# Hybrid decoder layer: the score products with the keys' low parts as pairs of 64-row matmuls

## The chip, the cores and the metric

The kernel runs on one core of a Trainium2 chip. The time is the device time of one execution in microseconds (us); where several executions are shown, the median is meant.

## The reference

One layer over 1040 positions (16 learned meta positions ahead of 1024 inputs), width 1024. After a norm and one input projection, head group B is a sliding-window attention (window 128) with 8 query heads of 64 channels over 2 key heads, and a sink value per head; group A is a convolution and a gated linear recurrence. Then come an output projection and a feed-forward block of width 4096. Cut to what matters here:

```
z = u @ w_in;  q, k, v, xr, yr = split(z)
s = einsum("bnqkgd,bnskd->bnkgqs", qb, kk) * 64**-0.5      # blocks of 128 queries x 256 keys
s = where(valid, s, -1e30);  m = max(max(s), sink)
p = exp(s - m);  o = einsum(..., p / (sum(p) + exp(sink - m)), vv)
a, gates:  r = sigmoid(einsum(x_blocks, w_a)), i = sigmoid(einsum(x_blocks, w_x))   # 8 blocks of 64 x 64
h = h + rmsnorm(concat(o, rec) @ w_out);  h = h + rmsnorm(relu(u @ w_ff1)**2 @ w_ff2)
```

## The kernel before

**Numbers in two parts.** TensorE (PE) works on rounded float32 (`F32R`). To keep accuracy, each operand is held as a high part (rounded) and a low part (what the rounding lost), and a product is made of high times high, high times low and low times high. The helper `mm3` records these as its three lines L125, L130 and L131, so most PE rows of the profile carry one of those lines.

**Queries and keys.** The heads are taken in pairs `j` of 0 to 3: query head `j` with key head 0 and query head `j + 4` with key head 1, `h` being 0 or 1. Key head `h` lies in partitions `HALF[h]` (0 to 63, or 64 to 127). For each pair and each `h`, the tile `q[h]` holds the high part of the query in `HALF[h]` and its low part in the other half. The tile `khh[h]` holds the high part of key head `h` in both halves (a DMA at L532 copies it across), so that one matmul over 128 rows gives high times high plus low times high. The tile `kl[h]` (L294) holds the low part of key head `h` in `HALF[h]` and zeros in the other half (two memsets on GpSimd, L297), so that a second matmul over 128 rows, with the same `q[h]`, adds high times low alone. `km` is a small tile of the same parts for block 0: slots 0 and 1 are high parts, slots 2 and 3 low parts with zeros (memsets L411, L412). The functions `low_k` and `sink_k` fill all these as the key projection leaves PSUM.

**Scores.** `scores(j, half, q)` computes 4 blocks of 128 queries against 256 keys for both `h`. For each `h`, and for each of two pairs of blocks `bp`, it takes a PSUM bank with the tag "s" (two banks have it), and puts into it for each of two blocks `i` the matmul of L625 (with `khh`) and that of L629 (with `kl`), each with a 128 x 128 stationary part of `q[h]` and 256 moving columns. ScalarE (ACT) and VectorE (DVE) take the bank out (L642, L643). After both `bp` of an `h` come its minimum (L652), four exponentials, the reciprocal and the scaling (L661). It runs 8 times, 4 `j` by 2 `half`: 64 matmuls of L625 and 64 of L629. `attend` then transposes the probabilities (L675) and multiplies them by the values (L691).

**What sets the order.** The program is written as one stream; a scheduler with its own timeline puts each engine's instructions in order, by priorities and the times that it expects. The remaining input projections (`next_fill`, of the `mm3` lines) are recorded with a lower priority (`deferred(FILL_LAG)`), so that the scheduler spreads them between the matmuls of scores and attention. At run time every engine keeps the order that was fixed. Tiles with one tag share a fixed number of buffers (17 for "b", in which `khh`, `kl`, `q` and later operands lie).

**Gates.** Later, `gates` multiplies 64-channel blocks: at L817 two matmuls, one with its operands in partitions 0 to 63, one in 64 to 127, write to two PSUM banks, three products in each of three column pieces (348, 348 and 344 columns), for four chunks `c`.

Of the kernel before, what the change touches and what calls it, by code (L numbers as in the profile page):

```python
# [10 lines left out]
F32R = mybir.dt.float32r  # L11
AF = mybir.ActivationFunctionType
ALU = mybir.AluOpType
# [3 lines left out]
P = 128  # L17
D = 1024
KC = D // P
T = 1024  # L20
NMETA = 16
# [16 lines left out]
def hybrid_layer(  # L38
# [6 lines left out]
    nc = tc.nc  # L45
# [12 lines left out]
    def slot(tag, shape, dt=F32):  # L58
        uid[0] += 1
        return slab.tile(shape, dt, tag=tag, name=f"{tag}{uid[0]}", bufs=bufs[tag])  # L60
# [4 lines left out]
    def bank(tag, shape=(P, 512)):  # L65
        uid[0] += 1
        return ps.tile(list(shape), F32, tag=tag, name=f"ps_{tag}{uid[0]}")

    def f32(ap):
        return ap.bitcast(F32)  # L70
# [10 lines left out]
    def lut(*args, **kwargs):  # L81
        ins = nc.scalar.activation(*args, **kwargs).ins  # L82
        if last_lut[0] is not None:
            tc.add_manual_dep(
                ins, last_lut[0],
                mybir.DependencyInfo(
                    mybir.DependencyClass.NoSync, mybir.DependencyReason.DATA
                ),
                reason="lut",
            )  # L90
        last_lut[0] = ins.name
        return ins
# [198 lines left out]


    khh = [slot("b", [P, T], F32R) for _ in range(2)]
    kl = [slot("b", [P, T], F32R) for _ in range(2)]  # L294
    HALF = (slice(0, HD), slice(HD, P))
    for h in range(2):
        nc.gpsimd.memset(f32(kl[h][HALF[1 - h]]), 0.0)  # L297

    zeros = slot("ws", [P, 512], F32R)
    nc.vector.memset(f32(zeros), 0.0)  # L300
# [30 lines left out]
    def chained(e, ins):  # L331
        if last[e] is not None:
            behind(last[e], ins)
        last[e] = ins.name
# [73 lines left out]
    wq = high_w(rq)  # L408
    low_w(wq, rq)
    km = slot("ws", [P, 4, 2 * P], F32R)  # L410
    nc.gpsimd.memset(f32(km[:, 0:2, 0 : P - NMETA]), 0.0)  # L411
    nc.gpsimd.memset(f32(km[:, 2:4, :]), 0.0)  # L412
    nsink = const.tile([P, 8], F32, name="nsink")
    nc.sync.dma_start(nsink, attn_sinks[0].partition_broadcast(P))
    prm_r = slot("d", [8, 512])
# [16 lines left out]
    def high_k(hh, src):  # L432
        return [nc.scalar.copy(hh[h][HALF[h]], src[HALF[h]]).ins for h in range(2)]

    def low_k(hh, lo, src):
        return [
            nc.vector.tensor_tensor(
                lo[h][HALF[h]], src[HALF[h]], f32(hh[h][HALF[h]]), op=ALU.subtract
            ).ins
            for h in range(2)  # L440
        ]

    def sink_k(acc, t0, n):
        o = NMETA if t0 == 0 else 0
        c = slice(t0 + o - NMETA, t0 - NMETA + n)
        parts = [([khh[0][:, c], khh[1][:, c]], [kl[0][:, c], kl[1][:, c]], acc[:, o:])]
        if o:

            m, mk = slice(0, NMETA + P), slice(P - NMETA, 2 * P)
            parts.append(  # L450
                ([km[:, 0, mk], km[:, 1, mk]], [km[:, 2, mk], km[:, 3, mk]], acc[:, m])
            )
        ops = [[], []]
        for hh, lo, src in parts:
            ops[0] += high_k(hh, src)
        for hh, lo, src in parts:
            ops[1] += low_k(hh, lo, src)
        if o:
            for e in range(2):
                for ins in ops[e]:  # L460
                    chained(e, ins)
# [36 lines left out]
    for b in range(4):  # L498
# [3 lines left out]
        if b == 0:  # L502

            acc = [bank("acc"), bank("acc")]
            for a, w in zip(acc, (wk, wv)):
                part(a, w, piece, 0)
                part(a, w, piece, 1)
            xn = [(norm_rows(xt[2], P, True), P)]
            xn.append((norm_rows(xt[3], P, True), P))
            part(acc[0], wk, piece, 2)  # L510
            sink_k(acc[0][:, : piece[1]], *piece)
            part(acc[1], wv, piece, 2)
            sink_v(acc[1][:, : piece[1]], *piece)
            wx = high_w(rx)
            low_w(wx, rx)
            for w, (t0, n), sink, tag in (
                (wq, (16, 256), sink_q0, "o"), (wx, piece, sink_x0, "acc"),
            ):
                acc = bank(tag)
                for k in range(3):  # L520
                    part(acc, w, (t0, n), k)
                sink(acc[:, :n], t0, n)
            done.append(last_mm[0])
            continue
        project(wk, [piece], sink_k)
        project(wv, [piece], sink_v)
        project(wq, [piece], sink_q0)
        project(wx, [piece], sink_x0)
        done.append(last_mm[0])
    for h in range(2):  # L530
        r, o, m = HALF[h], HALF[1 - h], slice(P - NMETA, 2 * P)
# [62 lines left out]
    for b in range(2):  # L594
        pv = bank("pt", (P, 4, P))
        for i in range(4):
            o = NMETA + (4 * b + i) * P
# [11 lines left out]
    def scores(j, half, q):  # L609

        sn = slot("c", [P, 2, 4, P + 1])
        negm = small.tile([P, 2, 4], F32, name="negm", tag="negm")
        den = small.tile([P, 2, 4], F32, name="den", tag="den")
        rden = small.tile([P, 2, 4], F32, name="rden", tag="rden")
        for h in range(2):
            nc.gpsimd.tensor_copy(
                sn[:, h, :, P], nsink[:, j + 4 * h : j + 4 * h + 1].to_broadcast([P, 4])
            )
        for h in range(2):
            for bp in range(2):  # L620
                sp_ = bank("s", (P, 2, 256))

                def qk(dst, b, hi, lo):
                    c = slice(b * P, (b + 1) * P)
                    nc.tensor.matmul(  # L625
                        dst, q[h][:, c], hi, start=True, stop=False,
                        skip_group_check=True,
                    )
                    nc.tensor.matmul(  # L629
                        dst, q[h][:, c], lo, start=False, stop=True,  # L630
                        skip_group_check=True,
                    )

                for i in range(2):
                    b = 4 * half + 2 * bp + i
                    if b == 0:
                        qk(sp_[:, i, :], b, km[:, h, :], km[:, 2 + h, :])
                    else:
                        c = slice((b - 1) * P, (b + 1) * P)
                        qk(sp_[:, i, :], b, khh[h][:, c], kl[h][:, c])  # L640
                s_ = sn[:, h, 2 * bp : 2 * bp + 2, 0:P]
                nc.scalar.copy(s_, sp_[:, :, P:256])  # L642
                nc.vector.copy_predicated(  # L643
                    s_, above_i.rearrange("p (a b) -> p a b", a=1).to_broadcast([P, 2, P]),
                    sp_[:, :, 0:P],
                )
                if half == 0 and bp == 0:
                    w = slice(0, P - NMETA)
                    nc.vector.copy_predicated(
                        sn[:, h, 0, w], above_i[:, w], far.to_broadcast([P, P - NMETA])  # L650
                    )
            nc.vector.tensor_reduce(  # L652
                negm[:, h, :], sn[:, h], axis=mybir.AxisListType.X, op=ALU.min
            )
            for k in range(4):
                lut(
                    sn[:, h, k, :], sn[:, h, k, :], AF.Exp, scale=-1.0,
                    bias=negm[:, h, k : k + 1], accum_out=den[:, h, k : k + 1],
                )
            nc.vector.reciprocal(rden[:, h, :], den[:, h, :])  # L660
            nc.vector.tensor_tensor(  # L661
                sn[:, h, :, 0:P], sn[:, h, :, 0:P],
                rden[:, h, :].to_broadcast([P, 4, P]), op=ALU.mult,
            )
        return sn
# [109 lines left out]
    for j in range(NPAIR):  # L775
        for half in range(2):
            if j % 2 == 0 and half == 0:
                at_pair(j // 2)
            gate_after = last_lut[0]
            sn = scores(j, half, qs[j])  # L780
            if True:
                with deferred(FILL_LAG):
                    next_fill()
            if prev is not None:
                attend(*prev)
            prev = (j, half, sn)
# [652 lines left out]
    def col_parts(i, j):  # L1439
        return HALVES if i == 6 and j == 3 else COLS[:1]  # L1440
# [32 lines left out]
    for j in range(4):  # L1473
        parts = col_parts(6, j)
# [34 lines left out]
```

## Time and profile before

| | us |
|---|---|
| median of 3 executions | 958.47 |
| the three | 956.39, 958.47, 961.83 |
| span of the profiled execution, first to last instruction | 955.3 |
| PE busy in it | 943.8 |
| PE weight loads (PEld) busy | 789.7 |
| DVE busy | 655.7 |
| ACT busy | 505.9 |
| GpSimd (POOL) busy | 129.1 |

For the profiled execution the profile gives the span and no separate time; the median of the shown executions is 3.2 us above that span. In a row of the timeline the first number is the start in us from the span's start, the second the duration in us, then the engine, the line, the operation, what it writes and reads, for matmuls the rows and columns of the stationary part (128\*128, 64\*128), and the shape of the moving operand. Matmuls are pipelined, so that rows overlap: what one costs PE is read from start to start, not from its duration.

### The profile page before, as it was taken

The page shows a single profiled execution, that of the slowest core. Times are in us where ns is not written, and L with a number is a line of the kernel's source. Part 1 is how long each engine was busy: PE and PEld are TensorE (multiplying, and loading weights), DVE is VectorE, ACT ScalarE, POOL GpSimd, SP SyncE. Part 2 cuts the span into 40 slices and gives each one's busy share as a digit, 9 for nine tenths or more (in the row PEclk, how much of TensorE's full clock was granted, in tenths as well). Part 3 has the DMA queues.
Part 4 walks back from the last instruction along what each step waited for, and adds up shares of the span by engine and source line. Part 5 has one row for each costly group of instructions (what it writes and reads, how often), then busy time and mean ns, then how long its engine had stood idle before and what let it go on. Part 6 is the DMA issues. An engine that isn't in the chain of part 4 may idle for free.

```text
span 955.3 us, 12432 instructions
## 1 busy us (share of the span) xinstructions
PE 943.8 (99%) x4728; PEld 789.7 (83%) x4728; DVE 655.7 (69%) x845; ACT 505.9 (53%) x854; POOL 129.1 (14%) x189
## 2 busy tenths in 40 slices
PE   9999999999999999999999999999999999999996
PEld 8999999877888878888888888888887788888885
DVE  6567987788856787665644465476667576779893
ACT  7537766568645554444655575654433343446441
POOL 4102563520021100010000000001121100001201
PEclk9999999999999999999999999999999999999999
DMA  8221010204226368674422364334777765647934
GB/s 271 56 67 23 24 45 24 67 23 131 83 109 185 133 220 264 198 253 144 155 89 88 111 203 127 104 113 114 175 180 186 185 199 177 192 139 196 246 65 89
DMA packets 88199, 130.21 MB, mean 136 GB/s; under 512 B 13702, under 2 KB 52630, under 8 KB 88140
## 3 DMA queue, kind: packets, MB, share of 16 engines
q1 hardware_dynamic: 78972, 104.44, 34.0%
q0 software_dynamic: 8880, 24.19, 12.2%
q8 instruction: 37, 0.61, 0.3%
q10 hardware_dynamic: 288, 0.79, 0.2%
q14 instruction: 22, 0.18, 0.1%
HBM read 109.93 MB, written 18.87 MB: 135 GB/s over the span
## 4 chain that ended last, share of the span: by engine, by line
PE 88%; DVE 5%; ACT 3%; DMA 2%; POOL 1%; issue 1%; SPq 0%; DVEq 0%; ACTq 0%; POOLq 0%
PE ps_acc L130 10%; PE ps_acc L131 10%; PE ps_acc L125 10%; PE ps_s L131 6%; PE ps_s L130 6%; PE ps_s L125 6%; PE ps_pt L130 6%; PE ps_pt L131 6%; PE ps_pt L125 6%; PE ps_o L130 5%; PE ps_o L131 5%; PE ps_o L125 5%; ACT c L82 1%; PE ps_o L691 1%; PE ps_acc L282 1%
## 5 line engine op out<-in xcount | busy, mean ns | idle before, releaser
L99 DVE TENSOR_TENSOR ws<-raw,ws 128x1024 fp32r<-128x1024 f32 (+1 forms) x69 | 82.6, 1197 | 76.1 <-ACT ws L96 24.3
L96 ACT CAST ws<-raw 128x1024 fp32r<-128x1024 f32 (+1 forms) x68 | 69.7, 1026 | 87.9 <-PE ps_o L130 23.9
L96 ACT CAST ws<-e 128x1024 fp32r<-128x1024 f32 x41 | 43.0, 1049 | 82.8 <-PE ps_o L130 35.3
L125 PE MATMUL ps_acc<-a,ws 128*128 128x256 f32 (+2 forms) x256 | 85.8, 335 | 0.0
L130 PE MATMUL ps_acc<-a,ws 128*128 128x256 f32 (+2 forms) x256 | 85.5, 334 | 0.0
L131 PE MATMUL ps_acc<-a,ws 128*128 128x256 f32 (+2 forms) x256 | 85.0, 333 | 0.0
L99 DVE TENSOR_TENSOR b<-b,b 128x1024 fp32r<-128x1024 f32 (+2 forms) x50 | 58.9, 1177 | 24.8 <-PE ps_o L130 19.1
L96 ACT CAST b<-b 128x1024 fp32r<-128x1024 f32 (+2 forms) x49 | 49.9, 1019 | 46.4 <-DVE b L996 41.0
L99 DVE TENSOR_TENSOR ws<-e,ws 128x1024 fp32r<-128x1024 f32 x41 | 50.1, 1223 | 32.4 <-ACT ws L96 18.9
L680 POOL TENSOR_SCALAR_AFFINE_SELECT c<-c 128x512 fp32r<-128x512 f32 x64 | 53.6, 858 | 67.6 <-ACT c L96 59.3
L125 PEld LDWEIGHTS ps_acc<-a,ws 128*128 128x128 f32 x256 | 48.3, 189 | 4.7 <-issue 0.2
L131 PEld LDWEIGHTS ps_acc<-a,ws 128*128 128x128 f32 x256 | 48.3, 189 | 4.5
L130 PEld LDWEIGHTS ps_acc<-a,ws 128*128 128x128 f32 x256 | 48.2, 188 | 4.4 <-issue 0.4
L125 PE MATMUL ps_acc<-ws,b 128*128 128x512 f32 (+1 forms) x120 | 46.3, 387 | 1.1 <-ACT ws L96 1.1
L130 PE MATMUL ps_acc<-ws,b 128*128 128x512 f32 (+1 forms) x120 | 46.3, 386 | 0.5 <-DVE ws L99 0.4
L131 PE MATMUL ps_acc<-ws,b 128*128 128x512 f32 (+1 forms) x120 | 46.1, 385 | 0.0
L125 PE MATMUL ps_pt<-ws,b 128*128 128x512 f32 x112 | 44.4, 396 | 0.0
L130 PE MATMUL ps_pt<-ws,b 128*128 128x512 f32 x112 | 44.1, 394 | 0.0
L131 PE MATMUL ps_pt<-ws,b 128*128 128x512 f32 x112 | 44.0, 393 | 0.0
L125 PE MATMUL ps_s<-ws,b 128*128 128x512 f32 x110 | 43.4, 395 | 0.0
L131 PE MATMUL ps_s<-ws,b 128*128 128x512 f32 x110 | 43.3, 394 | 0.0
L130 PE MATMUL ps_s<-ws,b 128*128 128x512 f32 x110 | 43.3, 393 | 0.0
(416 smaller groups left out, 2662.0 us busy)
## 6 DMA issues: line engine op xcount, KB each, us to landing
raw<-in_w_ff_dram SPq DMA_DIRECT2D x61, 512.0 KB, 4.1
e<-in_w_ff_dram SPq DMA_DIRECT2D x45, 512.0 KB, 4.0
a<-in_w_ff_dram SPq DMA_DIRECT2D x12, 512.0 KB, 6.6
s_dram<-a POOLq DMA_DIRECT2D x12, 512.0 KB, 3.7
c<-in_x_dram SPq DMA_DIRECT2D x8, 512.0 KB, 4.0
raw<-in_w_in_dram SPq DMA_DIRECT2D x8, 512.0 KB, 3.7
d<-in_x_dram SPq DMA_DIRECT2D x8, 512.0 KB, 3.3
out_dram<-raw SPq DMA_DIRECT2D x8, 512.0 KB
```

The source lines that it names most:

```text
L82: ins = nc.scalar.activation(*args, **kwargs).ins
L96: nc.scalar.copy(hi, src)
L99: low = nc.vector.tensor_tensor(lo, src, f32(hi), op=ALU.subtract).ins
L125: ins = nc.tensor.matmul(dst, lh, rh, start=start, stop=False, skip_group_check=True).ins
L130: nc.tensor.matmul(dst, lh, rl, start=False, stop=False, skip_group_check=True)
L131: last_mm[0] = nc.tensor.matmul(dst, ll, rh, start=False, stop=stop, skip_group_check=True).ins.name
L282: last_mm[0] = nc.tensor.matmul(acc[:, :n], w[k // 2][:, kc, :], u[kc][k % 2][:, t0 : t0 + n], start=k == 0 and kc == 0, stop=k == last an ...
L680: nc.gpsimd.affine_select(out=p_[:, :, s], in_=f32(p_[:, :, 0]), pattern=[[0, 4], [g, P]], compare_op=op, fill=0.0, base=0, channel_multip ...
L691: nc.tensor.matmul(po[:, oc : oc + n], v, p_[:, pc : pc + n], start=first and k == 0, stop=last and k == 1, skip_group_check=True,)
```

## The change

There is now one tile `kl`, with the low parts of both key heads, each in its own half, and no zeros; `km` needs three slots, the third with both low parts. In `scores` both `h` are handled together for each `bp`: two banks are taken, and for each block the order written is two matmuls with the high parts (128 rows, one for each `h`), then two with the low parts over 64 rows, from `HALF[0]` and `HALF[1]`, into the two banks. The two banks are then taken out, and the rest of the softmax follows in a second loop over `h`, after both `bp` of both heads. Three of the four memsets go; one of them becomes one slot longer.

```
-    kl = [slot("b", [P, T], F32R) for _ in range(2)]
+    kl = slot("b", [P, T], F32R)
     HALF = (slice(0, HD), slice(HD, P))
-    for h in range(2):
-        nc.gpsimd.memset(f32(kl[h][HALF[1 - h]]), 0.0)
...
-    nc.gpsimd.memset(f32(km[:, 0:2, 0 : P - NMETA]), 0.0)
-    nc.gpsimd.memset(f32(km[:, 2:4, :]), 0.0)
+    nc.gpsimd.memset(f32(km[:, 0:3, 0 : P - NMETA]), 0.0)
...
-                lo[h][HALF[h]], src[HALF[h]], f32(hh[h][HALF[h]]), op=ALU.subtract
+                lo[HALF[h]], src[HALF[h]], f32(hh[h][HALF[h]]), op=ALU.subtract
...
-        for h in range(2):
-            for bp in range(2):
-                sp_ = bank("s", (P, 2, 256))
...
+        for bp in range(2):
+            sps = [bank("s", (P, 2, 256)) for _ in range(2)]
+            for i in range(2):
+                b = 4 * half + 2 * bp + i
+                cq, ck = slice(b * P, (b + 1) * P), slice((b - 1) * P, (b + 1) * P)
+                for h in range(2):
                     nc.tensor.matmul(
-                        dst, q[h][:, c], hi, start=True, stop=False,
-                        skip_group_check=True,
+                        sps[h][:, i, :], q[h][:, cq],
+                        khh[h][:, ck] if b else km[:, h, :],
+                        start=True, stop=False, skip_group_check=True,
                     )
+                for h in range(2):
+                    r = HALF[h]
                     nc.tensor.matmul(
-                        dst, q[h][:, c], lo, start=False, stop=True,
-                        skip_group_check=True,
+                        sps[h][:, i, :], q[h][r, cq], kl[r, ck] if b else km[r, 2, :],
+                        start=False, stop=True, skip_group_check=True,
                     )
...
+            for h in range(2):
+                sp_ = sps[h]
                 s_ = sn[:, h, 2 * bp : 2 * bp + 2, 0:P]
                 nc.scalar.copy(s_, sp_[:, :, P:256])
...
+        for h in range(2):
             nc.vector.tensor_reduce(
                 negm[:, h, :], sn[:, h], axis=mybir.AxisListType.X, op=ALU.min
             )
```

In the changed kernel the matmuls with the high parts are L622 and those with the low parts L629.

More of the change, by code (lines that the diff above doesn't have):

```diff
@@ L445, in sink_k @@
         c = slice(t0 + o - NMETA, t0 - NMETA + n)
-        parts = [([khh[0][:, c], khh[1][:, c]], [kl[0][:, c], kl[1][:, c]], acc[:, o:])]
+        parts = [([khh[0][:, c], khh[1][:, c]], kl[:, c], acc[:, o:])]
         if o:
@@ L450, in sink_k @@
             parts.append(
-                ([km[:, 0, mk], km[:, 1, mk]], [km[:, 2, mk], km[:, 3, mk]], acc[:, m])
+                ([km[:, 0, mk], km[:, 1, mk]], km[:, 2, mk], acc[:, m])
             )
@@ L618, in scores @@
             )
-        for h in range(2):
-            for bp in range(2):
-                sp_ = bank("s", (P, 2, 256))
-                def qk(dst, b, hi, lo):
-                    c = slice(b * P, (b + 1) * P)
+        for bp in range(2):
[4 more added lines that the diff above has]
+                for h in range(2):
                     nc.tensor.matmul(
-                        dst, q[h][:, c], hi, start=True, stop=False,
-                        skip_group_check=True,
-                    )
+                        sps[h][:, i, :], q[h][:, cq],
+                        khh[h][:, ck] if b else km[:, h, :],
+                        start=True, stop=False, skip_group_check=True,
+                    )
+                for h in range(2):
+                    r = HALF[h]
                     nc.tensor.matmul(
-                        dst, q[h][:, c], lo, start=False, stop=True,
-                        skip_group_check=True,
-                    )
[L634 to L640, printed above, removed]
+                        sps[h][:, i, :], q[h][r, cq], kl[r, ck] if b else km[r, 2, :],
+                        start=False, stop=True, skip_group_check=True,
+                    )
+            for h in range(2):
+                sp_ = sps[h]
                 s_ = sn[:, h, 2 * bp : 2 * bp + 2, 0:P]
```

## The prediction

> **What bounds the kernel now.** I read the page first: how busy each engine is, the clock granted to PE, and the chain of work that ended last.
>
> ```profile
> span 955.3 us, 12432 instructions
> ...
> PE 943.8 (99%) x4728; PEld 789.7 (83%) x4728; DVE 655.7 (69%) x845; ACT 505.9 (53%) x854; POOL 129.1 (14%) x189
> ...
> PEclk9999999999999999999999999999999999999999
> ...
> PE 88%; DVE 5%; ACT 3%; DMA 2%; POOL 1%; issue 1%; SPq 0%; DVEq 0%; ACTq 0%; POOLq 0%
> ```
>
> PE is busy for 943.8 of 955.3 us at full clock, and holds 88% of the chain. A busy share is no proof, since matmul rows overlap, so I ask who made PE wait (the waits of PE; us in total, times, longest; the three that count).
>
> ```profile
> PE ps_acc L308 <- DVE base_e L562: 1.5, 1, 1.5
> PE ps_acc L125 <- ACT ws L96: 1.1, 1, 1.1
> ...
> PE ps_o L691 <- POOL c L680: 0.3, 1, 0.3
> ```
>
> The first is the program's start, the second is in the feed-forward part, and only the third, 0.3 us, is in the attention. The windows place the rest: scores and attention, everything behind the gates up to PE's last matmul, and the tail.
>
> ```profile
> core 0: us, PE busy (x) PEld busy (x) DVE busy (x) ACT busy (x) POOL busy (x), PEclk, DMA share, GB/s
> 59.70:196.00 136.30, 135.98 (x931) 125.60 (x930) 111.55 (x188) 87.65 (x251) 56.58 (x76) 1.00 0.16 43
> ...
> 212.00:948.10 736.10, 734.27 (x3246) 597.02 (x3244) 492.74 (x550) 372.79 (x500) 51.67 (x71) 1.00 0.53 156
> 948.10:955.30 7.20, 0.03 (x1) 0.00 (x0) 2.83 (x7) 0.20 (x1) 0.43 (x1) 0.77 0.71 159
> ```
>
> In the 136.30 us that hold the scores PE is idle for 0.32, and in the 736.10 us behind the gates for 1.83. So PE time that the change adds or removes in the scores moves the end by about as much: what can absorb an addition is at most 0.3 + 1.8 = 2.1 us, and I take it as nothing, since each of these waits has its own cause behind it.
>
> **The low products as they are.** One head's four block products in the timeline, the first two, the last, and the transpose that follows:
>
> ```profile
> 79.98 0.28 PE L625 MATMUL ps_s<-b,b 128*128 128x256 f32 x1
> 80.09 0.28 PE L629 MATMUL ps_s<-b,b 128*128 128x256 f32 x1
> ...
> 80.81 0.28 PE L629 MATMUL ps_s<-b,b 128*128 128x256 f32 x1
> 80.92 0.27 PE L675 MATMUL ps_pt<-ident,c 128*128 128x128 f32 x1
> ```
>
> Eight products take 80.92 - 79.98 = 0.94 us, 0.118 each. The 64 products of L629 cost 64 x 0.118 = 7.5 us, and if all ran as 32 pairs, two at once, 3.8 us would be saved. That is the most that pairing can bring, and it is under 0.5% of the time (4.8 us), about what a measurement of this kernel can tell from no change.
>
> **What a 64-row pair costs.** The kernel already has such pairs, in the gates (L817). One chunk, with the full-height projections (512 columns) on both sides:
>
> ```profile
> 209.19 0.39 PE L130 MATMUL ps_acc<-a,ws 128*128 128x512 f32 x1
> 209.42 0.39 PE L131 MATMUL ps_acc<-a,ws 128*128 128x512 f32 x1
> 209.74 0.43 PE L817 MATMUL ps_s<-b,e 64*128 64x348 f32 x1
> 209.75 0.43 PE L817 MATMUL ps_pt<-b,e 64*128 64x348 f32 x1
> 210.01 0.32 PE L817 MATMUL ps_s<-b,e 64*128 64x348 f32 x1
> ...
> 211.11 0.32 PE L817 MATMUL ps_pt<-b,e 64*128 64x344 f32 x1
> 211.12 0.32 PE L817 MATMUL ps_o<-b,e 64*128 64x344 f32 x1
> 211.37 0.50 PE L125 MATMUL ps_acc<-a,ws 128*128 128x512 f32 x1
> 211.71 0.39 PE L130 MATMUL ps_acc<-a,ws 128*128 128x512 f32 x1
> 211.94 0.39 PE L131 MATMUL ps_acc<-a,ws 128*128 128x512 f32 x1
> ```
>
> The pairs are real: both start within 0.01 us, and from the second pair (210.01) to the ninth (211.11) are seven steps of 0.157 us. A full-height product of 348 columns would cost, on a line through 0.118 at 256 columns and 0.23 at 512 (209.19 to 209.42), 0.158. So two 64-row products take the time of one full one, and a pair of 256 columns should take 0.118.
>
> The switch between full height and half height is what costs. From 209.42 to 211.71 are 2.29 us. The work in them is one 512-column product, nine pairs and one more 512-column product: 0.23 + 9 x 0.157 + 0.23 = 1.87. The rest, 0.42 us, is one way in and one way out. The first pair could have started at 209.65 and started at 209.74, and its rows are 0.43 long instead of 0.32; on the way out a start was due at 211.27, came at 211.37, and the row is 0.50 instead of 0.39. Each switch is thus about 0.10 us in which nothing starts, and 0.11 us in which the weights load with no product beside them. The weight loads show the second part:
>
> ```profile
> 209.74 0.18 PEld L817 LDWEIGHTS ps_s<-b,e 64*128 64x128 f32 x1 [0.36 <-ACT c L82]
> ...
> 209.85 0.19 PEld L817 LDWEIGHTS ps_s<-b,e 64*128 64x128 f32 x1
> ```
>
> After idling, the first load keeps its half of the array for 0.11 us before the next follows, at which time the first product streams. (The wait on ACT named there is older than the idle time: the product before ran until then.)
>
> The Trainium skill speaks against this change at this point: TensorEngine Tiling (Array Packing), Key Properties, says that changing the tiling mode, and not just the tile, drains the TensorE. It gives no duration; the 0.10 us in which nothing starts agree with it. TensorE: Matmul & The Clock Gate, LDWEIGHTS (loading the stationary operand), puts a load at its columns divided by 1.2, in ns; an estimate for 128 columns is 0.107 us. With that load alone at each switch the sum below would be 51 x 2 x 0.107 - 1.5 = 9.4 us.
>
> **How often it switches.** The diff writes two high, two low; the scheduler decides what stands where. In the order of the changed program (L622 high, L629 low; `b_268` and `b_269` are the two heads' queries):
>
> ```
> 513 L622 Matmult ps_s_1002<-b_109,b_268 128x256
> 514 L629 Matmult ps_s_1002<-b_111,b_268 128x256
> 515 L622 Matmult ps_s_1003<-b_110,b_269 128x256
> 516 L629 Matmult ps_s_1003<-b_111,b_269 128x256
> 517 L622 Matmult ps_s_1002<-b_109,b_268 128x256
> 518 L622 Matmult ps_s_1003<-b_110,b_269 128x256
> 519 L629 Matmult ps_s_1002<-b_111,b_268 128x256
> 520 L629 Matmult ps_s_1003<-b_111,b_269 128x256
> ```
>
> The second block is a pair; in the first the scheduler put each low product right behind its high one, alone between full-height products. Over all 64 low products there are 51 runs: 13 pairs of two different halves and 38 products alone. A product alone over 64 rows streams the same 256 columns and saves nothing.
>
> **The sum on PE.** 51 runs x 0.42 = +21.4 us (0.415 by the unrounded steps: +21.2); 13 pairs x 0.118 = -1.5. That is +19.6 us. The trace has no run of one product between full-height ones. Its bounds: below, the loads alone (0.11 at each switch), 51 x 0.22 - 1.5 = +9.7; above, the whole 0.42, +19.9. I take the upper row, since both parts of it come from the change of height and not from the number of products between.
>
> **What else moves.** The removed memsets are at the start:
>
> ```profile
> 1.12 0.95 POOL L297 MEMSET b<- 64x1024 f32 x1
> 2.40 0.94 POOL L297 MEMSET b<- 64x1024 f32 x1
> ...
> 4.72 0.57 POOL L176 TENSOR_TENSOR rs<-ms,half_pow 16x1 f32<-16x1 f32 x1
> 5.25 0.69 DVE L242 CUSTOM_DVE_ANT_0 d<-c 128x512 f32<-128x512 f32 x1 [3.77 <-DMA c<-in_x_dram]
> 5.86 0.74 DVE L260 TENSOR_SCALAR d<-d,rs 16x1024 f32<-16x1024 f32 x1
> ...
> 8.36 0.53 POOL L412 MEMSET ws<- 128x512 f32 x1
> ```
>
> The meta rows' norm (L176) ends at 5.29, and its reader on DVE (L260) stands behind L242, which waits for a DMA and holds DVE to 5.86. So an earlier L176 gives nothing: the DMA covers it, and 0. The memset at 8.36 has no reader on PE before the scores. The smaller `kl` frees one of 17 "b" buffers; among PE's waits none is for a buffer, so 0 again, at most the 2.1 us of idle time. DMA issues on SP stand in the same order; the other queues change only inside the attention.
>
> The new wait is in the softmax: head 0 can no longer start while head 1 is multiplied, and both finish together. The durations (x count, busy us, mean ns):
>
> ```profile
> L643 DVE COPY_PREDICATED c<-above,ps_s 128x256 f32<-128x256 int32 x32 | 13.0, 448 | 0.6 <-ACT c L642 0.2
> L661 DVE TENSOR_TENSOR c<-c,rden 128x512 f32<-128x512 f32 x15 | 11.0, 731 | 0.4
> L652 DVE TENSOR_REDUCE negm<-c 128x4 f32<-128x516 f32 x16 | 11.0, 685 | 0.5
> ...
> L82 ACT ACTIVATE c<-c,negm 128x129 f32<-128x129 f32 x64 | 25.0, 395 | 3.7 <-DVE negm L652 3.5
> ...
> L642 ACT COPY c<-ps_s 128x256 f32<-128x256 f32 x32 | 10.5, 373 | 2.6 <-PE ps_s L629 2.5
> ```
>
> From the last score product to the first transpose both heads need, if little overlaps, 0.37 + 2 x 0.45 + 2 x 0.69 + 8 exponentials at most 0.39 each + 2 x 0.73 = 7.3 us. In the changed order, with the steps above (0.118, 0.23, the switches), PE has at least 8.1 us of other work between the two in every one of the 8 score steps. The margin is 0.8 us, with DVE busy 111.55 of 136.30 us, so a wait is possible: 0 to about 0.6 us in each of 8 steps, 0 to 5 us. I take 0.
>
> **The rivals.**
> - *Only the weight load is exposed.* If the 0.10 us without a start came from changing a long stream of nine pairs and not from a single product, the sum is +9.7: 968. Against it: the delay is as long into the pairs as out of them.
> - *The softmax of two heads at once makes PE wait.* +19.6 and up to 5 more, 983. For it is the small margin; against it, PE is slower here, which gives ACT and DVE time.
> - *Not slower: the switch is hidden.* If the load for the other half slips under a running product, only 13 x 0.118 = 1.5 us of savings are left: 957. It decides where a way in and out costs less than 0.03 us; up to (4.8 + 1.5) / 51 = 0.12 us it stays within 0.5%. The Trainium skill, TensorE: Matmul & The Clock Gate, Part 3, has a rule for it: loads overlap products in flight where the row group differs. The gates' 0.42 us show that it does not hold between full and half height, since a full-height product uses every row.
> - *The change does not do what it says:* 38 of 64 low products do not stand in pairs. This is part of my sum.
>
> **How the numbers follow.** The sum is against the span of 955.3, which would be 974.9; the median shown is 3.2 above that span, so I forecast 958.5 + 19.6 = 978. Chances: forecast 0.75; load alone 0.10; softmax waits 0.08; hidden switch 0.05; a gain over 0.5% 0.02, for what I do not see, since pairing brings 3.8 at most. The range 970 to 984 takes in a somewhat cheaper switch (0.28 us a run gives 971) and the softmax waits, and leaves out 0.17. Slower by over 0.5%: 0.75 + 0.10 + 0.08 = 0.93; within it 0.05; faster 0.02.
>
> **What would show it.** In the timeline after, a full-height product behind a lone low product should stream some 0.53 us (0.118 + 0.42) after that low product was due, with rows 0.11 us longer at each switch, and the window from the first score to the gates should be about 20 us longer, everything behind it the same. The forecast is wrong if that distance is near 0.12 us, if 64-row rows do not lengthen, or if the longer time lies in PE waits on ACT or DVE.

## The result and the profile after

The changed kernel takes 973.51 us (median of 4, 973.35 to 974.25) against 958.0 us (median of 4, 956.39 to 961.83) for the kernel before. The ratio is 1.017, with a 95% interval of 1.0149 to 1.019. It is slower by 15.5 us, inside the range and 4.5 us under the forecast.

The page of the changed kernel, the same lines as before:

```profile
span 971.9 us, 12425 instructions
...
PE 962.1 (99%) x4728; PEld 794.7 (82%) x4728; DVE 656.8 (68%) x845; ACT 507.9 (52%) x854; POOL 119.4 (12%) x186
...
PEclk9999999999999999999999999999999999999999
...
PE 92%; DVE 3%; DMA 2%; ACT 1%; issue 1%; DVEq 0%; SPq 0%; ACTq 0%
```

PE is busy 18.3 us longer (962.1 against 943.8) at the same clock, with the same 4728 matmuls; its part of the chain rises from 88% to 92%. DVE and ACT do what they did, within 2 us, and POOL is 9.7 us less busy (119.4 against 129.1), with three memsets fewer and 64 mask operations of 732 ns instead of 858 on average. The list of PE's waits is shorter than before, and none of them is in the attention:

```profile
PE ps_acc L306 <- DVE base_e L559: 1.5, 1, 1.5
PE ps_acc L125 <- ACT ws L96: 0.6, 1, 0.6
PE ps_pt L130 <- DVE a L99: 0.2, 1, 0.2
```

To place the time I cut both traces at the same matmuls: the 441st (which both programs have at the same place, 0.6 us ahead of the first score product before), the first of the gates, and PE's last. The windows before:

```profile
59.13:196.62 137.49, 137.17 (x938) 126.38 (x937) 112.14 (x192) 87.90 (x251) 56.67 (x77) 1.00 0.16 43
196.62:947.80 751.18, 749.35 (x3352) 609.06 (x3352) 505.12 (x563) 382.48 (x521) 55.70 (x73) 1.00 0.52 153
```

and after (columns: length, then the busy time of PE, PEld, DVE, ACT, POOL, clock, DMA):

```profile
58.57:213.71 155.14, 155.14 (x938) 130.92 (x936) 113.32 (x192) 89.57 (x251) 49.06 (x77) 1.00 0.14 38
213.71:964.30 750.59, 749.64 (x3352) 609.24 (x3352) 505.38 (x563) 382.80 (x521) 55.44 (x73) 1.00 0.53 154
964.30:971.90 7.60, 0.29 (x3) 0.08 (x1) 2.83 (x7) 0.20 (x1) 0.68 (x1) 0.86 0.74 160
```

Scores and attention take 155.14 us instead of 137.49, +17.65, with the same 938 matmuls. The scores start 0.56 us earlier, the part behind them is 0.59 shorter, the tail 0.1 longer: +16.6, the difference of the spans. (The 938 are all matmuls that touch the window; 936 start in it.) One of the score steps in the timeline shows the cost (128\*128 is full height, 64\*128 half height; "x2" is two products):

```profile
74.24 0.28 PE L622 MATMUL ps_s<-b,b 128*128 128x256 f32 x1
74.45 0.39 PE L629 MATMUL ps_s<-b,b 64*128 64x256 f32 x1
74.76 0.39 PE L622 MATMUL ps_s<-b,b 128*128 128x256 f32 x1
75.08 0.38 PE L629 MATMUL ps_s<-b,b 64*128 64x256 f32 x1
75.39 0.50 PE L622 MATMUL ps_s<-b,b 128*128 128x256 f32 x2
75.82 0.39 PE L629 MATMUL ps_s<-b,b 64*128 64x256 f32 x2
76.14 0.50 PE L125 MATMUL ps_acc<-a,ws 128*128 128x512 f32 x1
76.47 0.39 PE L130 MATMUL ps_acc<-a,ws 128*128 128x512 f32 x1
```

Where high and low alternate, the steps are 0.31 us (74.45, 74.76, 75.08, 75.39) instead of 0.118: each change of height costs 0.19. It has two parts that can be read from the rows. The low product was due at 74.36 and starts at 74.45, and its row is 0.39 long where the high one's is 0.28. The weight loads go with this. Between full-height products, here before the change, the load for the product at 62.15 starts 0.11 us ahead of it, with the product before:

```profile
62.04 0.28 PE L131 MATMUL ps_acc<-a,ws 128*128 128x256 f32 x1
62.04 0.19 PEld L125 LDWEIGHTS ps_acc<-a,ws 128*128 128x128 f32 x1
62.15 0.28 PE L125 MATMUL ps_acc<-a,ws 128*128 128x256 f32 x1
```

At a change of height, after the change, the load starts only with its own product (at 74.45 and 74.76):

```profile
74.44 0.18 PEld L629 LDWEIGHTS ps_s<-b,b 64*128 64x128 f32 x1 [0.25 <-issue]
74.76 0.19 PEld L622 LDWEIGHTS ps_s<-b,b 128*128 128x128 f32 x1
```

The pair at 75.82 streams in the time of one product, as in the gates, but pays the same way in and out.

### The profile page after: what moved, and what is told of

Same layout as the page of the kernel before. It is cut to its first block, busy times and chain, and to the rows that moved or that the text cites. A ratio compares the mean times of both kernels' runs of the same rounds, so it can differ in the third digit from the quotient of the medians.

```text
span 971.9 us, 12425 instructions
## 1 busy us (share of the span) xinstructions
PE 962.1 (99%) x4728; PEld 794.7 (82%) x4728; DVE 656.8 (68%) x845; ACT 507.9 (52%) x854; POOL 119.4 (12%) x186
## 4 chain that ended last, share of the span: by engine, by line
PE 92%; DVE 3%; DMA 2%; ACT 1%; issue 1%; DVEq 0%; SPq 0%; ACTq 0%
PE ps_acc L130 11%; PE ps_acc L131 11%; PE ps_acc L125 11%; PE ps_s L131 6%; PE ps_s L130 6%; PE ps_s L125 6%; PE ps_pt L130 6%; PE ps_pt L131 6%; PE ps_pt L125 6%; PE ps_o L130 5%; PE ps_o L131 5%; PE ps_o L125 5%; PE ps_o L686 2%; PE ps_s L629 2%; PE ps_s L622 1%; PE ps_acc L282 1%
## 5 line engine op out<-in xcount | busy, mean ns | idle before, releaser
L99 DVE TENSOR_TENSOR ws<-raw,ws 128x1024 fp32r<-128x1024 f32 (+1 forms) x69 | 82.8, 1200 | 75.8 <-ACT ws L96 24.7
L96 ACT CAST ws<-raw 128x1024 fp32r<-128x1024 f32 (+1 forms) x68 | 69.8, 1026 | 86.4 <-PE ps_o L130 26.9
L96 ACT CAST ws<-e 128x1024 fp32r<-128x1024 f32 x41 | 43.0, 1049 | 81.6 <-PE ps_o L130 34.0
L99 DVE TENSOR_TENSOR b<-b,b 128x1024 fp32r<-128x1024 f32 (+2 forms) x50 | 58.9, 1178 | 24.8 <-PE ps_o L130 19.1
L96 ACT CAST b<-b 128x1024 fp32r<-128x1024 f32 (+2 forms) x49 | 50.0, 1020 | 46.8 <-DVE b L991 41.4
L99 DVE TENSOR_TENSOR ws<-e,ws 128x1024 fp32r<-128x1024 f32 x41 | 50.1, 1222 | 32.3 <-ACT ws L96 18.9
L675 POOL TENSOR_SCALAR_AFFINE_SELECT c<-c 128x512 fp32r<-128x512 f32 x64 | 45.1, 732 | 95.1 <-ACT c L96 92.6
```

The source lines that it names most:

```text
L96: nc.scalar.copy(hi, src)
L99: low = nc.vector.tensor_tensor(lo, src, f32(hi), op=ALU.subtract).ins
L675: nc.gpsimd.affine_select(out=p_[:, :, s], in_=f32(p_[:, :, 0]), pattern=[[0, 4], [g, P]], compare_op=op, fill=0.0, base=0, channel_multip ...
```

## The experiments

Two theories. "Switch": every run of half-height products between full-height ones costs PE a fixed time for the way in and out, whatever is in it. "Order": the time comes from the new loops, with both heads at once, the softmax starting later, and another order by the scheduler. For each kernel stand the total, and the window from the 441st matmul to the first gate, in which PE's busy time is set against the 137.17 us of before.

**Full height in the new order.** The loops of the changed kernel stay, and the zeros come back:

```
+    kl = [slot("b", [P, T], F32R) for _ in range(2)]     # zeros in the other half
...
-    sps[h][:, i, :], q[h][r, cq], kl[r, ck] if b else km[r, 2, :],
+    sps[h][:, i, :], q[h][:, cq], kl[h][:, ck] if b else km[:, 2 + h, :],
```

> The changed kernel with its loops and PE order kept, its low products put back to full height with zeros in the other half (64 products alone or in pairs at the same 51 places). Theory 'switch' (each run of half-height products costs PE about 0.39 us for the way in and out, whatever is computed): nothing of the 16 us is left, 957 to 959 us, and PE's steps in the scores are 0.118 us throughout. Rival 'order' (both heads at once, the softmax starting later and the scheduler's new order cost the time): as slow as the changed kernel, 972 to 975 us.

Measured: 957.12 us (956.2 to 959.65) against 956.0 for the kernel before in the same session, ratio 1.0011 (0.9999 to 1.0023). All matmuls stand in the order of the changed kernel, and the instructions of ACT and DVE too. Its window, a step of the same form as 75.39 to 76.14 above, and its longest PE wait in the attention:

```profile
58.91:197.38 138.47, 137.34 (x938) 126.17 (x936) 112.04 (x192) 88.79 (x251) 49.43 (x77) 1.00 0.16 43
```

```profile
65.84 0.48 PE L625 MATMUL ps_s<-b,b 128*128 128x256 f32 x2
66.16 0.40 PE L631 MATMUL ps_s<-b,b 128*128 128x256 f32 x2
66.40 0.39 PE L125 MATMUL ps_acc<-a,ws 128*128 128x512 f32 x1
```

```profile
PE ps_acc L125 <- DVE b L479: 0.9, 1, 0.9
```

Two low products take 0.24 us, and PE's busy time is back to 137.34. This kernel differs from the changed one in the height of 64 products, the second tile of low parts and the memsets, and its window is 16.7 us shorter (138.47 against 155.14). "Order" falls; what is left of it is a PE wait of 0.9 us on DVE, which the slower products had covered. The tile and the memsets go with the height here, but all kernels below have one tile and no zeros, like the changed one, and PE's busy time grows by 3.7 to 24.4 us in them, with the number of runs. So the height is the cause.

**Half height in the old order.** The loops of before, with the shared tile, and each low product behind its own high one:

```
-    dst, q[h][:, c], lo, start=False, stop=True,
+    dst, q[h][HALF[h], c], lo, start=False, stop=True,
```

> The kernel before with its loops, but one tile of low parts and half-height low products: each of the 64 stands alone behind its high product, so there are 64 runs and no pair. 'Switch': 64 x 0.39 = +25.0 us and about -0.5 at the start without the memsets, 982 to 983 us. 'Order': the loops are those of before, so 957 to 959 us. A third theory, that a half-height product costs something only where two write two banks at once and a lone one is cheaper: under 974 us.

Measured: 979.85 us (978.59 to 982.15), ratio 1.0251 (1.0234 to 1.0267), +23.9, where +24.5 was expected. (The total is 2 us under the range expected, which counted from 958, while the kernel before, timed beside it, took 956.0.) Its window, and the first steps of a score group:

```profile
58.84:220.44 161.60, 161.60 (x938) 134.03 (x936) 115.47 (x192) 90.25 (x251) 52.32 (x77) 1.00 0.14 37
```

```profile
66.22 0.38 PE L626 MATMUL ps_s<-b,b 64*128 64x256 f32 x1
66.53 0.39 PE L622 MATMUL ps_s<-b,b 128*128 128x256 f32 x1
66.85 0.38 PE L626 MATMUL ps_s<-b,b 64*128 64x256 f32 x1
67.16 0.39 PE L622 MATMUL ps_s<-b,b 128*128 128x256 f32 x1
```

No pair is in it, and it is the slowest: a lone half-height product pays in full. The third theory falls too.

**All 32 pairs together.** The low products are ordered behind the second high one of their block:

```
+    low = nc.tensor.matmul(...).ins
+    behind(high.name, low)
```

> The changed kernel with each low product ordered behind the second high product of its block, so that all 32 pairs stand together (32 runs of two). 'Switch': 32 x 0.39 - 32 x 0.118 = +8.7 us, with -0.5 at the start 966 us (965 to 968). 'Order': the loops and the softmax are as late as in the changed kernel, 972 to 975 us.

Measured: 965.14 us (964.36 to 966.87), ratio 1.0097 (1.008 to 1.0114), +9.1. Its window:

```profile
58.84:204.98 146.14, 145.90 (x940) 126.44 (x938) 112.53 (x191) 88.24 (x251) 51.33 (x77) 1.00 0.15 41
```

This is the form that the change's words describe, and it is still slower: a pair saves 0.118 us and pays more than three times that.

**Runs of four.** The high products of both blocks first, then the low ones of both:

```
             for i in range(2):
                 ...  # both high products
+            for i in range(2):
                 for h in range(2):
                     low = ...
+                    behind(high.name, low)
```

> The changed kernel with the low products of two blocks ordered behind their last high product: 19 runs, 14 of them of two pairs, 3 of one pair, 2 of one product. 'Switch': 19 x 0.39 - 31 x 0.118 = +3.8 us, with -0.5 at the start 961 us (960 to 963); if a longer run cost more than one way in and out, above 966 us. 'Order': 972 to 975 us.

Two sums are open in one bank here at once, each with a mark of its start, and the output is off by 0.14 (relative); the kernel is read for its time only. Measured: 969.23 us (966.65 to 970.09), ratio 1.0132 (1.0115 to 1.015), +13.2: a miss by 8 us. By the total alone the other theory named there, that a longer run costs more (above 966), would hold. The window to the gates decides against it:

```profile
58.81:200.70 141.89, 140.85 (x937) 125.08 (x936) 110.73 (x188) 84.99 (x247) 51.34 (x77) 1.00 0.15 42
```

It is 4.4 us longer than before, where +3.8 was expected, and PE's busy time in it is 3.7 longer. (One projection of 512 columns, 0.23 us, stands behind the first gate here and not ahead of it; with it the two are 4.6 and 3.9.) From the first gate to PE's last matmul, however, it takes 760.1 us instead of 751.2. The next two kernels were made for that.

**Runs of four in half of the steps.** Steps with `half == 1` have runs of four, the others pairs; behind the scores the order is that of the 32 pairs.

> Steps of the first half keep pairs (as with 32 pairs), steps of the second half order the low products of two blocks together: 26 runs, 7 of four products, 1 of three, 15 of two, 3 of one, so 30 pairs that share. Behind the scores the PE order is that of the kernel with 32 pairs for its last 3250 matmuls. 'Switch' at 0.38 us a run (the three runs so far: 0.377 for 64, 0.376 for 51, 0.388 for 32): 26 x 0.38 - 30 x 0.118 = +6.3 us from the first scores to the gates, 962 to 963 us in all, between 32 pairs (965.1) and the kernel before. If runs of four were what made the kernel with 19 runs slow (969.2), this one would be at or above 965.

Measured: 964.46 us (963.12 to 969.79) against 956.46, ratio 1.0092 (1.0067 to 1.0117), +8.0. The expected 962 to 963 was missed by 1.5 to 2.5 us. It stayed under 965 by half a microsecond, which its executions, 6.7 us apart, do not tell from the 965.14 of the 32 pairs; the window does:

```profile
59.21:203.70 144.49, 143.85 (x939) 126.09 (x937) 112.54 (x191) 87.26 (x250) 50.11 (x77) 1.00 0.15 41
```

The window is 7.0 us longer, of which 0.3 is more idle time (0.64 against 0.32); PE's busy time is 6.7 longer for 6.3 expected, and 2.05 shorter than with 32 pairs. So runs of four are not dearer.

**19 runs, one start per bank.**

```
-    start=True, stop=False, skip_group_check=True,
+    start=i == 0, stop=False, skip_group_check=True,
```

> The kernel with 19 runs again, in the same order of instructions, but with the second block's first product not marked as the start of a sum. If the time of the 19 runs lies in the scores as their count says (+4 us to the gates) and the rest in the order that the scheduler chose behind them (PE waits after the gates), it repeats: 967 to 970 us, with the gates at 200.7 us. If the sums that were open at once in a bank slowed PE, it is 961.

Measured: 969.95 us (969.26 to 973.36), ratio 1.0147 (1.0125 to 1.0169). It repeats, with the first gate at 200.88, so the sums open at once in a bank did not slow PE. With one start per bank the output is whole again. Its waits of PE behind the gates, and two windows there:

```profile
PE ps_pt L131 <- DVE b L99: 1.9, 2, 1.0
PE ps_acc L125 <- ACT ws L96: 1.8, 1, 1.8
...
PE ps_pt L125 <- ACT b L96: 1.2, 1, 1.2
```

```profile
265.00:275.00 10.00, 6.93 (x23) 4.66 (x22) 8.38 (x12) 3.91 (x8) 0.00 (x0) 0.84 0.22 65
272.00:276.00 4.00, 3.77 (x10) 3.03 (x11) 1.38 (x3) 1.18 (x3) 0.00 (x0) 0.60 0.76 254
```

The scheduler put the work behind the scores in another order. In the timeline the gates stand in 8 groups instead of 4, which is four more ways in and out (some 1.6 us); PE idles for 3.1 of 10 us while ACT and DVE finish the recurrence; and behind that idle time the granted clock is 0.60 for 4 us, some 1.6 us of lost work. With the 1.8 us wait later, which was 1.1 before, this is about 7 of the 9 us, and the projection that stands behind the first gate is 0.23; the rest I did not place.

**The price of a run.** PE's busy time in the window over that of before, plus 0.118 for each pair that shares, divided by the runs (for the runs of four with the 0.23 us of the projection missing in its window):

| kernel | PE busy, us | runs | pairs | us a run |
|---|---|---|---|---|
| full height, new order | +0.17 | 0 | 0 | - |
| half height, old order | +24.43 | 64 | 0 | 0.382 |
| the changed kernel | +17.97 | 51 | 13 | 0.382 |
| 32 pairs | +8.73 | 32 | 32 | 0.391 |
| runs of four in half | +6.68 | 26 | 30 | 0.393 |
| runs of four | +3.68 | 19 | 31 | 0.398 |

Five kernels with 19 to 64 runs of one to four products give the same price to within 0.016 us, 0.38 to 0.40. That it depends on the number of runs and not on what is in them is shown, for runs of one to four of these products.

## Why the prediction was right

**PE is the bound, and nothing absorbs an addition.** Right. PE's busy time in the window grew by 17.97 us and the window by 17.65: the 0.32 us of idle time in it are gone. Everything behind it shrank by 0.59: PE's largest wait there, on ACT at L96, went from 1.1 to 0.6, and the 0.4 us on DVE at L99 is gone.

**The switch.** Right in kind: no start, then a load that begins with its own product and not with the one before, on the way in and on the way out. The size was 0.42 us a run from the gates, 0.415 in the sum; measured 0.382. On the way in the start is 0.09 late (0.10 forecast) and the row 0.10 longer (0.11); from the low product's due start at 74.36 to the stream of the next high one (74.76 and 0.10) are 0.50 us, where 0.53 was forecast. Why the gates' run was dearer stays open. This term was sized 1.7 us too high: 51 x (0.415 - 0.382). The Trainium skill, TensorEngine Tiling (Array Packing), Key Properties, names the drain at a change of mode, and the traces put 0.09 to 0.10 us on it in both directions; the load alone, which was a rival at 968, is little over half the price (0.22 of 0.38 us).

**51 runs and 13 pairs.** Right: the timeline after has them as the order of the program had them. A forecast from the diff alone, 32 pairs, would have been +9.5 by the prediction's terms, 32 x (0.415 - 0.118), or 968; the third experiment measured +9.1 for that form.

**The start costs nothing.** Not refuted. In the profiled executions the scores of the changed kernel start 0.56 us earlier, but this is not shown to be the change's doing. 0.14 of it is a DMA that landed earlier (L242 starts at 5.10 instead of 5.25; in the other kernels between 5.28 and 5.66). The rest lies between L242 and the 441st matmul, 53.89 us before and 53.46 after; see the last section. The experiments counted 0.5 us for the memsets that are gone, and it did not come: in the five kernels without them the 441st matmul starts between 0.32 us earlier and 0.08 later than before.

**Idle time behind the scores.** I took what it could absorb as nothing; it gave 0.59 us. From the first gate to PE's last matmul the kernel with full height and the one with 64 lone products both take 749.8 us, 1.4 less than before, so that a difference of this size is not shown to come from the slower scores.

**The median.** I added the sum to the median shown, 3.2 us above the profiled span. An execution's time is 1.7 to 2.1 us above its own span in the runs on record, so the profiled execution was some 1.5 us faster than the median. For the changed kernel the median, 973.51, is 1.6 us above the span of 971.9. These 1.6 us with 1.7 for the switch, 0.3 for the idle time in the scores, 0.56 and 0.59, less 0.1 for the longer tail, make up the 4.5 us to the rounding. They are small, from different causes, and that nearly all lie in one direction is chance as far as is known.

**The rivals.** The load alone (968) and the hidden switch (957) are ruled out by the price of a run. Waits of the softmax did not come: PE does not wait in the attention at all. Where the products are fast again (first experiment) the new loops make PE wait 0.9 us once, for a projection's bank: ACT (L476) and DVE (L479) empty it only after the exponentials of both heads. The margin that the prediction worked out, from the last score product to the first transpose, was wider than it looked. In that kernel's shortest such stretch, 157.78 to 164.11, PE has 6.33 us of other work and does not wait, and DVE has scaled both heads at 163.18, after 5.4 us, where the prediction, with little overlap, counted 7.3:

```profile
157.78 0.28 PE L631 MATMUL ps_s<-b,b 128*128 128x256 f32 x1
...
162.49 0.69 DVE L659 TENSOR_TENSOR c<-c,rden 128x512 f32<-128x512 f32 x1
...
164.11 0.60 PE L673 MATMUL ps_pt<-ident,c 128*128 128x128 f32 x4
```

In the changed kernel the shortest such stretch is 8.05 us (170.76 to 178.81), as the prediction's 8.1 had it.

## What to carry to other kernels

Half-height products between full-height ones cost a way in and out, here 0.38 us, while a pair of 256 columns saves 0.118: an estimate from these two is that four pairs have to stand together before anything is won; in the gates nine do. Count the changes of height in the order that the scheduler made, not in the source. And when a small reordering moves the total by more than its own stage, cut the traces at common instructions first: the rest may be another order further down.

## What the runs showed of the hardware

The granted clock of PE can fall after several short waits. In the kernel with 19 runs and one start per bank, waits of 1.2, 1.0 and 0.9 us within 4.8 us were followed by 4 us at a mean clock of 0.60 (0.57 in the other kernel with 19 runs, after 1.6, 1.0 and 0.9 us). A single wait of 1.8 us, later in the same kernel (769.5 to 771.3 us), left it at 1.00:

```profile
771.00:775.00 4.00, 3.57 (x14) 2.65 (x15) 3.50 (x3) 3.17 (x4) 0.00 (x0) 1.00 0.33 103
```

That the waits made the clock fall is read from this order of events; no run varied them alone.

A DVE operation and GpSimd memsets met at the start, and the one or the other became longer. Before, beside the memset of 0.53 us at 8.36, two DVE operations took 1.26 us:

```profile
8.29 1.26 DVE L248 TENSOR_SCALAR d<-c,rs 128x512 f32<-128x512 f32 x2
```

After, they took 0.91, and the memsets beside them were the longer ones (0.44 us for the memset of `vmt`, 0.20 before):

```profile
8.13 0.91 DVE L248 TENSOR_SCALAR d<-c,rs 128x512 f32<-128x512 f32 x2
8.31 0.44 POOL L585 MEMSET vmt<- 128x128 f32 x1 [3.24 <-PE ps_o L160]
8.70 0.65 POOL L409 MEMSET ws<- 128x336 f32 x1
```

PE waits for L248 there (0.6 us in the list of waits before), and the 0.35 us between the two fit most of the 0.42 us between L242 and the 441st matmul. The memsets alone do not decide it. The first experiment has them all back, and there L248 takes 0.89 us:

```profile
8.01 0.53 POOL L412 MEMSET ws<- 128x512 f32 x1
8.46 0.89 DVE L248 TENSOR_SCALAR d<-c,rs 128x512 f32<-128x512 f32 x2
```

From L242 to the 441st matmul it takes 53.50 us, in the six kernels without them 53.45 to 53.56. In the first experiment the memset is nearly over when L248 starts, so that the moment at which they meet may decide; no run varied that alone.
